# Start offsets of SBUF tiles: three unused tiles ahead of the large ones in a Griffin-style encoder layer

## The chip, the cores and the metric

The kernel runs on one core of one Trainium2 chip. The metric is the device time of one execution in microseconds (us). Five engines work from their own instruction streams: TensorE (PE; its weight loads are listed apart as PEld), VectorE (DVE), ScalarE (ACT), GpSimd (POOL) and SyncE (SP), which here only issues transfers. SBUF has 128 partitions; a tile takes the same range of bytes in each of them, and "offset" below is where that range begins. Times are in us, durations of single instructions in ns.

## The reference

One layer over 1024 frames of width 1024, in float32: RMSNorm, one combined projection, two attention branches, a gated merge, an output projection and a squared-ReLU feed-forward, then a final RMSNorm.

```python
h = rms_norm(x, norm1[l])
proj = h @ w_in[l]
qa, ka, va, fa, qc, kc, vc, gates = jnp.split(proj, SPLITS, axis=-1)
o_a = forgetting_attention(qa, ka, va, cumsum(log_sigmoid(fa + forget_bias)))   # 8 heads x 64, causal
o_b = chunk_band_attention(qc, kc, vc, rel_bias)                                # 8 heads x 64, 640 keys
g_a, g_b = jnp.split(jax.nn.sigmoid(gates), 2, axis=-1)
merged = g_a * (o_a @ w_branch_a) + g_b * (o_b @ w_branch_b)
x = x + merged @ w_out
x = x + jnp.square(jax.nn.relu(rms_norm(x, norm2) @ w_up)) @ w_down             # 1024 -> 4096 -> 1024
return rms_norm(x, final_norm)
```

(Calls are shortened; head reshapes and casts are left out.)

## The kernel before

**Arithmetic.** Each float32 operand of a product is split into a high part, rounded to the matmul's float32r, and the low rest. A product is three matmuls of 128x128 weights with 128x512 moving columns: high x high, low x high, high x low (line 216). ScalarE makes the high part by a cast (lines 163 and 278), VectorE or GpSimd the low part by a subtraction (lines 165 and 279). The large projections use Strassen's scheme with seven products in place of eight, so sums and differences of weights (names S, ks, ka) and of activations (T1 to T4) are formed too.

**Stages.** Opening: x is loaded in tiles of 128x512 (xg), scaled, split and combined into the operands B11 to T4, while the first gates and the forget projection f are multiplied; the same x, laid out by rows, is loaded into the tiles n0, n1 and the two halves of rstd in turn and squared (line 312) for the first norm. Then the projections of q, k, v and the gates (to about 420 us), attention over 16 heads (to about 650 us; scores s from qk and sk, exponentials p, transposes pt, their parts th and tl, weighted sums pv), the branch and output projections, the up projection with its activations stored to DRAM (to about 1112 us), and the down projection, which reads them back, with the final norm and the output.

**Order of work.** A scheduler at build time puts the instructions of each engine in order, from the program and a model of durations; operations called through the wrappers VO, TO, AO, GO, LO keep the order of the program (line 106 in the profile). In attention strings of letters (FOX_HEAD and the like) set the order by hand. Each engine runs its stream in order and waits on semaphores; SP, ACT and POOL each have a queue of transfers, all served by the same 16 DMA engines.

**Where tiles lie.** Pools are opened on one of two sides. Those on the left are stacked upward from the low end of SBUF, those on the right downward from the top, and a pool that is closed gives its range to the next one opened on its side. A tile begins where the tile before it in its pool ends, rounded up to 32 bytes. Left: cpool (constants and rstd, line 117), tp (eight temporary tiles of 2048 bytes, line 118), then the operands, etile and, in the down projection, the raw and split activations, weights and sums. Right: wp (weights raw and split, line 119, open to the end), then the tiles of the q, k, v stage (epb) and all of attention (aps, apq0, app, apq1, apv, ap0). Tiles of 512 bytes and more are multiples of 256 bytes long, so one small tile early in a stack sets the offset, modulo 256, of all that follow. cpool holds an unused tile of 128 bytes, gap, just ahead of rstd. Offsets of the tiles of 512 bytes or more, modulo 256:

| tiles | offset before |
|---|---|
| left side after cpool: tp (tmp, z, m, vt), xg, B11 to T4, u, zt, qk, v and at, xB, xT, ka, ks, acc | 224 |
| right side: wp (wr, wh, wl, S), epb (qkh, qkl, vs), bc, mh and ml | 224 |
| right side, attention from wide downward: wide, qk and sk operands, p, v, th, tl, on, lo, mv, rb | 32 |
| rstd | 192 |
| ident | 128 |

The weights of the forget projection are the exception within a tile: 40 columns each, 160 bytes apart in one slice of T4h (line 380), so the eight of them start at eight different offsets.

Of the kernel before, what the change touches and what calls it, by code (L numbers as in the profile page):

```python
# [11 lines left out]
F32 = mybir.dt.float32  # L12
# [6 lines left out]
P = 128  # L19
# [73 lines left out]
def hybrid_block(ctx: ExitStack, tc: tile.TileContext, xT, xN, g1, wall, wf, fb, relb, g2, g3, outT):  # L93
# [17 lines left out]
    def pool(stack, name, side, bufs=1, **kw):  # L111
        return stack.enter_context(tc.tile_pool(name=name, bufs=bufs, side=side, reuse_waits="tile", **kw))
# [3 lines left out]

    cpool = pool(ctx, "cpool", "left")
    tp = pool(ctx, "tp", "left")
    wp = pool(ctx, "wp", "right")
    dpool = ctx.enter_context(tc.tile_pool(name="dpool", bufs=1, space=DRAM))  # L120

# [12 lines left out]

    cpool.tile([P, 32], F32, tag="gap", name="gap")
    rstd = cpool.tile([P, S], F32, tag="rstd", name="rstd")

    def dram(name, shape, dt=F32):
        return dpool.tile(shape, dt, tag=name, name=name)
# [510 lines left out]
    bstack.close()  # L650
    aps = pool(astack, "aps", "right")
    wide = aps.tile([P, S], F32, tag="wide", name="wide")
    G.memset(wide, 0.0)
    G.affine_select(out=wide[:, S - P:S], in_=wide[:, S - P:S], compare_op=ALU.is_ge, fill=-BIG, base=0, pattern=[[-1, P]],
                    channel_multiplier=1)
# [691 lines left out]
```

## Time and profile before

| | |
|---|---|
| median of 3 runs | 1427.92 us (1427.64 to 1430.43) |
| profiled execution, its own time | 1430.48 us |
| its span, first to last instruction | 1428.5 us |
| granted TensorE clock, mean | 0.995 |
| instructions in the span | 20411 |
| moved to and from DRAM | 259.75 MB in 132820 packets, mean 182 GB/s |

The span is what the profile covers; 2.0 us of the execution's own time lie around it. A group's row in the profile gives line, engine, operation, output <- inputs, shape and count, then busy time and mean of one, then the idle time ahead of it and who ended that. A matmul's duration there is its way through the array, and successive matmuls overlap: what the next one waits for is the distance of their starts. Rows that begin with minimum/median/maximum come from the view of one line or one tile.

### The profile page before, as it was taken

What the parts mean: (1) busy time and instruction counts of PE and PEld (TensorE: products, weight loads), DVE (VectorE), ACT (ScalarE), POOL (GpSimd) and SP (SyncE); (2) the same over time, 40 slices, a digit from 0 to 9 for tenths busy, and PEclk for the clock granted to TensorE, in tenths of its full rate; (3) what the DMA queues carried; (4) which work ended last, traced back from release to release, by engine and by line L of the source; (5) the groups of instructions that cost most, each with busy time, mean ns of one, the idle gap of its engine ahead of it and who ended that gap; (6) DMA issues with size and microseconds to landing.
All of it is one profiled execution on the core that took longest, in us unless ns stands there. A gap on an engine that the chain in (4) does not pass through costs nothing.

```text
span 1428.5 us, 20411 instructions
## 1 busy us (share of the span) xinstructions
PE 1400.7 (98%) x6676; PEld 1168.7 (82%) x6676; DVE 885.1 (62%) x1389; ACT 706.6 (49%) x1361; POOL 812.2 (57%) x639
## 2 busy tenths in 40 slices
PE   9999999999999999999999999999999999999996
PEld 6788888888878888888888888888888888888885
DVE  7756445543258887776655855545555559998644
ACT  8534333343358887775454543333333444444653
POOL 0477777778832233113724677777777545567564
PEclk9999999999999999999999999999999999999998
DMA  8546667773454668886644244444444784678263
GB/s 282 154 116 194 187 196 219 204 198 121 147 169 147 185 209 248 246 257 215 213 162 146 68 166 151 155 154 157 148 154 169 252 269 156 178 234 225 81 221 118
DMA packets 132820, 259.75 MB, mean 182 GB/s; under 512 B 18594, under 2 KB 20642, under 8 KB 129642
## 3 DMA queue, kind: packets, MB, share of 16 engines
q1 hardware_dynamic: 84570, 172.79, 38.6%
q10 hardware_dynamic: 44944, 77.78, 17.2%
q0 software_dynamic: 3200, 7.88, 2.5%
q8 instruction: 52, 0.85, 0.2%
q14 instruction: 54, 0.44, 0.1%
HBM read 172.70 MB, written 85.69 MB: 181 GB/s over the span
## 4 chain that ended last, share of the span: by engine, by line
PE 87%; DVE 3%; issue 3%; ACT 2%; POOL 2%; DMA 2%; SPq 0%; POOLq 0%; ACTq 0%; DVEq 0%
PE u L216 44%; PE dS L216 12%; PE dA L216 5%; PE o L216 5%; PE s L106 5%; PE pv L106 4%; PE pt L106 3%; PE m L106 3%; PE m L216 3%; POOL wl_A L165 1%; PE u L106 1%; DMA xg<-xT 1%; DMA xT<-a_dram 1%; ACT p L106 1%; PE vtp L627 0%
## 5 line engine op out<-in xcount | busy, mean ns | idle before, releaser
L165 POOL TENSOR_TENSOR wl_A<-wr,wh_A 128x512 fp32r<-128x512 f32 x118 | 158.4, 1352 | 94.0 <-ACT wh_A L163 77.0
L165 POOL TENSOR_TENSOR wl_S<-S,wh_S 128x512 fp32r<-128x512 f32 x102 | 136.0, 1337 | 32.9 <-ACT wh_S L163 32.3
L163 ACT CAST wh_S<-S 128x512 fp32r<-128x512 f32 x105 | 64.6, 621 | 114.0 <-PE u L216 53.9
L163 ACT CAST wh_A<-wr 128x512 fp32r<-128x512 f32 x105 | 65.0, 620 | 88.7 <-PE u L216 55.8
L106 DVE TENSOR_TENSOR tl<-pt,th 128x512 fp32r<-128x512 f32 (+1 forms) x144 | 90.5, 641 | 25.9 <-ACT th L106 24.4
L165 POOL TENSOR_TENSOR wl_S<-ks,wh_S 128x512 fp32r<-128x512 f32 x48 | 69.1, 1501 | 53.4 <-ACT wh_S L106 50.0
L590 DVE TENSOR_TENSOR u<-u,u 128x512 f32<-128x512 f32 x70 | 48.8, 698 | 76.0 <-PE u L216 73.6
L106 ACT ACTIVATE p<-s,mn 128x640 f32<-128x640 f32 (+3 forms) x120 | 84.4, 703 | 16.6 <-DVE mn L106 15.5
L106 ACT CAST th<-pt 128x512 fp32r<-128x512 f32 (+1 forms) x144 | 77.6, 551 | 24.5 <-PE pt L106 22.3
L106 PE MATMUL pt<-ident,p 128*128 128x128 f32 x528 | 78.1, 274 | 1.2 <-DVE zt L403 1.1
L186 POOL TENSOR_TENSOR S<-wr,wr 128x512 f32<-128x512 f32 x35 | 46.3, 1324 | 54.8 <-DMA wr<-wall 50.2
L106 PEld LDWEIGHTS pt<-ident,p 128*128 128x128 f32 x528 | 62.2, 141 | 11.0 <-PE pv L106 2.0
L106 PE MATMUL s<-qk 128*128 128x384 f32 (+2 forms) x192 | 58.6, 360 | 8.1 <-ACT p L106 7.3
L165 POOL TENSOR_TENSOR wl_A<-ka,wh_A 128x512 fp32r<-128x512 f32 x32 | 45.1, 1419 | 35.6 <-ACT wh_A L106 34.1
L278 ACT CAST qkh<-qk 128x512 fp32r<-128x512 f32 x32 | 19.9, 621 | 87.5 <-DMA qk_dram<-qkl 34.2
L1102 ACT ACTIVATE v<-v 128x512 f32<-128x512 f32 x64 | 40.4, 632 | 45.1 <-DVE v L1101 42.9
L924 POOL TENSOR_TENSOR on<-on,lo 128x512 f32<-128x512 f32 x7 | 9.0, 1292 | 92.7 <-ACT lo L106 92.7
L106 PE MATMUL pv<-th,v 128*128 128x512 f32 (+3 forms) x180 | 61.3, 348 | 0.1
L583 DVE TENSOR_TENSOR u<-u,c 128x512 f32<-128x512 f32 x35 | 24.5, 699 | 59.4 <-PE u L216 57.3
L106 PE MATMUL pv<-tl,v 128*128 128x512 f32 (+3 forms) x180 | 56.8, 335 | 0.2 <-DVE tl L106 0.2
L1101 DVE SCALAR_TENSOR_TENSOR v<-u,rstd 128x512 f32<-128x512 f32 x64 | 43.9, 688 | 20.1 <-PE u L216 18.1
L581 DVE TENSOR_TENSOR c<-u,u 128x512 f32<-128x512 f32 x35 | 24.2, 691 | 50.7 <-PE u L216 48.9
(445 smaller groups left out, 4742.2 us busy)
## 6 DMA issues: line engine op xcount, KB each, us to landing
wr<-wall SPq DMA_DIRECT2D x233, 256.0 KB
a_dram<-at ACTq DMA_DIRECT2D x64, 256.0 KB
xT<-a_dram SPq DMA_DIRECT2D x64, 256.0 KB
qk<-qk_dram SPq DMA_DIRECT2D x15, 1024.0 KB
qk_dram<-qkh ACTq DMA_DIRECT2D x96, 128.0 KB
a_dram<-v ACTq DMA_DIRECT2D x48, 256.0 KB
xB<-a_dram SPq DMA_DIRECT2D x44, 256.0 KB
z_dram<-zt ACTq DMA_DIRECT2D x32, 256.0 KB
```

Of the source, the lines that this page charges most:

```text
L106: return lambda *a, **kw: tc.keep_in_program_order(getattr(self.eng, name)(*a, **kw))
L163: (act.tensor_copy if act is G or act is V else act.copy)(wh, src)
L165: lows.append(eng.tensor_tensor(wl, src, wh.bitcast(F32), op=ALU.subtract))
L186: eng.tensor_tensor(t, raw(3), raw(2), op=ALU.add)
L216: done = eng.matmul(bank, w[wi], x[xi], start=(first and t == 0), stop=(t == n - 1 and not part), skip_group_check=part or not first)
L278: A.copy(dst[0], src)
L581: V.tensor_tensor(c22, banks[2], u2, op=ALU.add)
L583: V.tensor_tensor(banks[1], banks[3], c22, op=ALU.add)
L590: V.tensor_tensor(banks[b], banks[b], u2, op=ALU.add)
L924: G.tensor_tensor(o, o, lows_o[pr], op=ALU.add)
L1101: V.scalar_tensor_tensor(v, src, 0.0, rstd[:, hs(h)], op0=ALU.max, op1=ALU.mult)
L1102: A.activation(v, v, AF.Square)
```

## The change

Three tiles that nothing uses are added. A pool "edge" with 96 bytes (24 float32) is opened on the right ahead of wp, so that it lies at the top of SBUF; cpool gets 32 bytes (8 float32) behind rstd; aps gets 64 bytes (16 float32) behind wide.

```diff
     cpool = pool(ctx, "cpool", "left")
     tp = pool(ctx, "tp", "left")
+    pool(ctx, "edge", "right").tile([P, 24], F32, tag="shim", name="shim")
     wp = pool(ctx, "wp", "right")
...
     cpool.tile([P, 32], F32, tag="gap", name="gap")
     rstd = cpool.tile([P, S], F32, tag="rstd", name="rstd")
+    cpool.tile([P, 8], F32, tag="shim", name="shim")
...
     aps = pool(astack, "aps", "right")
     wide = aps.tile([P, S], F32, tag="wide", name="wide")
+    aps.tile([P, 16], F32, tag="shim", name="shim")
```

Left tiles behind rstd move up by 32 bytes, right tiles move down by 96, and those from wide downward by 96 + 64 = 160. In the two programs every instruction, its place on its engine, its semaphores and the counts that it waits for are the same; the SBUF offsets in the operands are what differs. Modulo 256 they become:

| tiles | before | after |
|---|---|---|
| left side after cpool | 224 | 0 |
| right side | 224 | 128 |
| attention from wide downward | 32 | 128 |
| rstd | 192 | 192 |
| ident | 128 | 128 |

Modulo 128, then, all large tiles stand at 0 but rstd, which stands at 64. The small tiles of cpool and aps behind the new ones (sums of the norms, minima and denominators of the softmax) move by 32, 96 or 160 bytes as well.

## The prediction

> **What bounds the kernel now.** I read the busy times first, then the chain of waits, then the stages one by one. The page's first part and its chain:
>
> ```profile
> PE 1400.7 (98%) x6676; PEld 1168.7 (82%) x6676; DVE 885.1 (62%) x1389; ACT 706.6 (49%) x1361; POOL 812.2 (57%) x639
> PE 87%; DVE 3%; issue 3%; ACT 2%; POOL 2%; DMA 2%; SPq 0%; POOLq 0%; ACTq 0%; DVEq 0%
> PE u L216 44%; PE dS L216 12%; PE dA L216 5%; PE o L216 5%; PE s L106 5%; PE pv L106 4%; PE pt L106 3%; PE m L106 3%; PE m L216 3%; POOL wl_A L165 1%; PE u L106 1%; DMA xg<-xT 1%; DMA xT<-a_dram 1%; ACT p L106 1%; PE vtp L627 0%
> ```
>
> TensorE is busy for 98% of the span and is 87% of the chain. All other engines and the transfers share the remaining 13%. The stages say where that rest lies (columns: duration, busy time and instructions of PE, its weight loads, DVE, ACT, POOL, then granted clock, DMA share, GB/s):
>
> ```profile
> 0.00:50.00 50.00, 44.83 (x187) 33.44 (x188) 41.62 (x76) 40.75 (x85) 3.28 (x8) 1.00 0.66 224
> 330.00:440.00 110.00, 106.04 (x494) 87.83 (x494) 48.82 (x91) 50.15 (x98) 62.42 (x51) 0.98 0.46 147
> 440.00:900.00 460.00, 453.39 (x2406) 386.61 (x2404) 326.35 (x603) 282.44 (x588) 202.00 (x153) 1.00 0.60 187
> 900.00:1000.00 100.00, 100.00 (x443) 82.84 (x442) 49.13 (x68) 38.56 (x64) 77.14 (x59) 1.00 0.45 153
> 1180.00:1428.00 248.00, 236.62 (x1088) 196.94 (x1086) 183.95 (x217) 117.85 (x211) 143.89 (x111) 0.98 0.57 173
> ```
>
> Between 900 and 1000 us PE never pauses. The pauses are 5.2 us in the opening, 4.0 us where attention begins, 6.6 us in the 460 us after that, and 11.4 us in the last stretch, most of it the tail after the last products. So a change can reach the end in two ways only: by what a matmul itself takes, or through about 28 us of pauses.
>
> **The change part by part.** *The three tiles.* Nothing writes or reads them, so they issue no instruction. The order of instructions, the semaphores waited on and the counts waited for are the same in both programs on all five engines; buffers are numbered differently, and the start offsets in SBUF differ. No step is moved past a queue and no wait is added. Direct cost: 0 us. What is left is the offsets. Tiles on the left side stood at 224 modulo 256 and come to 0; those on the right at 224 or (attention) 32, and come to 128; the 4 KB tile rstd stays at 192, so "all large tiles" is one short. The question is whether any instruction or transfer sees that. Tiles at 32, 192 and 224 already work side by side, and comparing them is the nearest thing the trace has to the change.
>
> *TensorE.* Its weight is the largest: every nanosecond on each of 6676 matmuls is 6.7 us (6676 x 1 ns). Two stretches, one with all operands at 224 (the up projection) and one with operands at 32 (scores in attention), columns being start, duration, engine and line:
>
> ```profile
> 1000.05 0.39 PE L216 MATMUL u<-T1h,wl_S 128*128 128x512 f32 x1
> 1007.08 0.39 PE L216 MATMUL u<-B22h,wh_S 128*128 128x512 f32 x1
> 605.36 0.39 PE L106 MATMUL s<-qk 128*128 128x512 f32 x1
> 605.59 0.39 PE L106 MATMUL s<-sk 96*128 96x512 f32 x1
> 605.82 0.38 PE L106 MATMUL pt<-ident,p 128*128 128x128 f32 x2
> ```
>
> From 1000.05 to 1007.08 there are 31 steps, so one matmul starts every 0.227 us; at 605.36 the steps are 0.23 and 0.23. Start offset 32 and start offset 224 give one pitch within the 10 ns that these rows resolve on a single step. Weight loads say the same, at 32 (v), at 224 (wh_g), and for 40-column slices of T4h that lie 160 bytes apart and so start at 224, 128, 32, 192, 96, 0 and on modulo 256:
>
> ```profile
> L106 PEld LDWEIGHTS pv<-th,v 128*128 128x128 f32 x180 | 34.0, 189 | 3.3 <-ACT th L106 0.3
> L371 PEld LDWEIGHTS g<-B21h,wh_g x8: 187/188/188, 16.3 to 22.5; 128*128 128x128 f32 x8
> L386 PEld LDWEIGHTS f<-B22h,T4h x4: 114/114/114, 26.8 to 37.9; 128*40 128x40 f32 x4
> L386 PEld LDWEIGHTS f<-B12l,T4h x4: 115/115/116, 25.2 to 36.3; 128*40 128x40 f32 x4
> ```
>
> 189 against 188 ns, and 114 to 116 ns for offsets that include 0 and 128, the two that the change brings. I take 0 ns for a matmul. As bounds I keep one nanosecond either way, which is the difference of the two full weight loads: -6.7 to +6.7 us.
>
> *ScalarE, VectorE, GpSimd.* One line squares tiles n (224) and rstd (192) in turn; on DVE and on POOL an operation with one or two SBUF operands stands at 32 (on) and at 224 (z, wl_ab) (minimum, median, maximum in ns):
>
> ```profile
> L312 ACT ACTIVATE n<-n x8: 614/625/635, 20.8 to 36.3; 128x512 f32<-128x512 f32 x8
> L312 ACT ACTIVATE rstd<-rstd x8: 615/624/635, 22.6 to 39.0; 128x512 f32<-128x512 f32 x8
> L106 DVE TENSOR_TENSOR on<-pv,mv x16: 677/683/696, 437.1 to 647.2; 64x512 f32<-64x512 f32 x16
> L106 DVE TENSOR_TENSOR z<-m,z x16: 680/681/692, 552.7 to 661.7; 128x512 f32<-128x512 f32 x16
> L873 POOL TENSOR_TENSOR on<-on,rb x14: 1267/1290/1306, 451.8 to 633.5; 128x512 f32<-128x512 f32 x14
> L757 POOL TENSOR_TENSOR wl_ab<-wrab,wh_ab x8: 1270/1292/1297, 535.7 to 648.9; 128x512 fp32r<-128x512 f32 x8
> ```
>
> The medians differ by 1 ns of 625, 2 of 683 and 2 of 1290, at most 0.3%. These engines are 3 + 2 + 2 = 7% of the chain, 100 us; 0.3% of that is 0.3 us, either way. I take 0. What hides the rest of their work is TensorE's 87%; where that cover is missing, the 28 us of pauses, it would cost 0.1 us.
>
> *Transfers.* In the opening SP issues two loads of 256 KB into n (224), then two into rstd (192); counted through the queue at 128 packets of 2 KB a tile, the packets of n run from 18.2 to 19.6 us and those of rstd from 19.5 to 20.9. The transfers within 18.3 to 19.4 and within 19.6 to 20.8:
>
> ```profile
> 15.05 1.00 SPq L106 DMA_DIRECT2D n<-xN  x2
> 16.41 1.01 SPq L106 DMA_DIRECT2D rstd<-xN  x2
> DMA packets 234, 0.42 MB, mean 384 GB/s; under 512 B 28, under 2 KB 28, under 8 KB 234
> DMA packets 253, 0.46 MB, mean 384 GB/s; under 512 B 28, under 2 KB 28, under 8 KB 253
> ```
>
> 384 GB/s for both, with the engines full. A start on a multiple of 64 (192) is worth nothing over one on 32 (224). No large transfer in this trace starts at 0 or 128, so this stays a bound: the nearest row says 0%. The far end goes by how many blocks a row of 2048 bytes touches: off a boundary of 128 it is 17 blocks in place of 16 (1/17, 6%), off a boundary of 256 it is 9 in place of 8 (1/9, 11%), and the latter is mended for left tiles alone, since right ones come to 128. The chain holds 2% of transfers, 29 us, so the far end is -3.2 us; a loss has no mechanism in these rows, and I keep the same 3.2 us for it. I take 0.
>
> *Sum.* 0 + 0 + 0 + 0 = 0. The profiled execution took 1430.48 us (span 1428.5 and 2.0 around it) and stands 2.56 us above the median of the three runs shown, 1427.92. No change to the one is no change to the other: **1427.9 us**.
>
> **The rivals.**
>
> *Transfers see a boundary* (faster). For it: every large transfer now starts off both boundaries, and afterwards only those of rstd start off 128. Against a boundary of 128: nothing direct, but n and rstd are equal although only rstd stands on a multiple of 64. Against one of 256: nothing, since n and rstd both miss it. Times: with 128 bytes 1427.9 - 1.7 = 1426.2, within 0.2%; with 256 bytes, if every transfer on the chain is one of the left side, 1427.9 - 3.2 = 1424.7, just beyond.
> The Trainium skill, page "DMA: Bandwidth & Descriptors", section "How a descriptor splits into AXI transactions", has a rule that speaks for the change: a transaction that reads must begin on a multiple of 256 bytes, and a descriptor that does not is charged the bytes before its start. As an estimate from that page, and if it held for the SBUF side of loads as well, 2048 bytes would cost 71 beats at 224, 70 at 192, 68 at 128 and 64 at 0, so left transfers would shorten by 10% and right ones by 4%. By that rule n and rstd should differ by 1.4%; the two rows above show no difference, though that is near what so short a window can tell.
>
> *TensorE streams faster from an aligned start* (faster). The mechanism: a matmul's fixed part contains a fetch that an aligned start saves. For it: 512 columns start every 0.227 us and 256 columns every 0.12, as the two ends of three steps near the end show, so 0.013 us of each matmul is fixed (2 x 0.12 - 0.227):
>
> ```profile
> 1414.86 0.28 PE L106 MATMUL dA<-xT4l,wh_A 128*128 128x256 f32 x1
> 1415.22 0.28 PE L106 MATMUL dA<-xT4l,wh_A 128*128 128x256 f32 x1
> ```
>
>  Against it: it is the same pitch at 32 and 224, and the T4h slices load in one time at every offset. Each nanosecond saved is -6.7 us; from 0.43 ns on it shows (2.86 / 6.7). With 1 ns: 1421.2 us.
>
> *Both sides meet on one weight port* (slower). Left tiles move to 0, right tiles to 128, while both stood at 224; the moving operand comes from the left and the weights from the right. If a load of weights and the stream under it then disturb each other, the weight load of 188 ns grows. It is hidden under the matmul before it until it passes 227 ns, so it decides from +39 ns; each nanosecond beyond is +6.7 us, and 1 ns beyond gives 1434.6 us. Against it: weight loads from v (32), wh_g (224) and the T4h slices show no dependence on where the two stand to each other.
>
> *It doesn't do what it says.* rstd keeps 192, and it is read by every scaling on DVE. If rstd alone carried the cost, nothing would move: 1427.9 again, the same number for another reason.
>
> **How the numbers follow.** What a measurement can tell here is about 0.2%, 2.86 us; the three runs shown lie 2.79 us apart. No effect at all, with rstd's case: 0.67, at 1427.9, own range 1425.5 to 1430.5. Transfers with 128 bytes 0.06 (same), with 256 bytes 0.06 (faster). TensorE faster: 0.09. Weight port: 0.06 (slower). The remaining 0.06 is for offsets that act through something I have not named: 0.02 faster, 0.04 slower, since no row excludes a loss there. Sums: faster 0.06 + 0.09 + 0.02 = 0.17; same 0.67 + 0.06 = 0.73; slower 0.06 + 0.04 = 0.10. The range takes in the transfers' gain and their loss, and most of TensorE's bound on the side of the gain: 1422.5 to 1431.5 us. Left out are the weight port, part of the unnamed and the far part of TensorE's gain, together under 0.2.
>
> **What would show it.** Right: 6676 matmuls and the same 0.227 us pitch; weight loads at 188 ns; ACT at 620 to 625 ns for 128x512 squares from a tile that now stands at 0; the xN loads still at 384 GB/s into n and rstd alike; the chain still 87% PE. Wrong: a pitch that is not 0.227 (TensorE), a rate for n that parts from rstd's (transfers, decided by n at 0 or 128 against rstd at 192 in one trace), or weight loads over 190 ns. A time outside 1425.1 to 1430.8 with all those rows equal would mean that offsets act through something that I have not named.

## The result: slower by 1.6%

| | before | after |
|---|---|---|
| median | 1428.66 us (1427.64 to 1430.43) | 1451.97 us (1450.48 to 1452.36) |
| profiled execution, span | 1428.5 us | 1448.6 us |
| granted TensorE clock, mean | 0.995 | 0.997 |

(Medians of five runs each.) After over before is 1.0158, with a 95% interval from 1.0146 to 1.0169: 23.3 us more by the medians, 20.1 us more by the two spans. The profiled execution of before, 1430.48 us, was its longest, and that of after, 1450.48 us, its shortest, which makes the 3.2 us between the two differences. The forecast was 1427.9 us, 1422.5 to 1431.5.

The page of the profile after, its busy times and its chain of waits:

```profile
PE 1421.5 (98%) x6676; PEld 1167.8 (81%) x6676; DVE 889.0 (61%) x1389; ACT 706.2 (49%) x1361; POOL 809.4 (56%) x639
PE 88%; DVE 4%; issue 3%; ACT 2%; POOL 1%; DMA 1%; SPq 0%; POOLq 0%; ACTq 0%; DVEq 0%
```

PE's busy time has grown by 20.8 us, with the same 6676 matmuls. Its weight loads, ACT and POOL have not grown, and DVE's 3.9 us lie beside PE. The 100 us of the up projection in which PE never pauses (columns as in the prediction) now hold 434 matmuls in place of 443, at the full clock:

```profile
900.00:1000.00 100.00, 100.00 (x434) 81.20 (x433) 48.84 (x67) 38.06 (x63) 74.22 (x57) 1.00 0.42 148
```

To place the time I cut both spans at the same matmuls, from the first of a stage to the first of the next, and took in each stage the mean distance from one start of a 512-column matmul to the next, over the distances below 260 ns (longer ones hold a pause or a record that is missing):

| stage | matmuls | before, us | after less before, us | distance before, ns | after, ns |
|---|---|---|---|---|---|
| opening | | 37.15 | +0.20 | | |
| projections of q, k, v, gates | 1630 | 363.76 | +8.54 | 227.0 | 233.1 |
| first scores | | 18.02 | +0.11 | | |
| attention | 1454 | 244.50 | -1.64 | | |
| branch projections | 192 | 43.60 | +1.25 | 226.8 | 233.3 |
| out projection | 384 | 87.04 | +0.02 | 226.7 | 226.7 |
| up projection | 1376 | 310.85 | +6.02 | 226.7 | 231.6 |
| down projection | 1411 | 313.30 | +5.68 | 226.7 (dS) | 232.4 (dS) |

Four stages lose 21.5 us, and the out projection, built in the same way with weights that are split in the same way, loses nothing. (The down projection of before holds one pause of about 1.3 us, at 1406 us where PE waits for wl_A, which the profile after has not, nor those with all tiles at 0 and at 128; without it the four lose 22.8 us, near the 23.3 of the medians.) Its rows are the control. The groups of one form, before and then after (the last numbers are busy time, mean ns of one, and the idle time ahead of it):

```profile
L216 PE MATMUL u<-T4h,wh_A 128*128 128x512 f32 x136 | 52.9, 389 | 0.0
L216 PE MATMUL o<-mh,wh_o 128*128 128x512 f32 x128 | 49.8, 389 | 0.0
L216 PE MATMUL dS<-xT1l,wh_S 128*128 128x512 f32 x64 | 24.9, 389 | 0.0
```

```profile
L218 PE MATMUL u<-T4h,wh_A 128*128 128x512 f32 x136 | 53.5, 394 | 0.0
L218 PE MATMUL o<-mh,wh_o 128*128 128x512 f32 x128 | 49.8, 389 | 0.0
L218 PE MATMUL dS<-xT1l,wh_S 128*128 128x512 f32 x64 | 25.2, 395 | 0.0
```

389 ns becomes 394 and 395, except for o. The timeline of after shows what that means for the next matmul:

```profile
760.01 0.39 PE L218 MATMUL o<-ml,wh_o 128*128 128x512 f32 x1
763.87 0.39 PE L218 MATMUL o<-mh,wh_o 128*128 128x512 f32 x1
1200.31 0.40 PE L218 MATMUL dS<-xT1h,wh_S 128*128 128x512 f32 x1
1203.81 0.40 PE L218 MATMUL dS<-xT1h,wh_S 128*128 128x512 f32 x1
```

Seventeen steps of the out projection take 3.86 us, 0.227 each; fifteen of the down projection take 3.50 us, 0.233 each. The longer steps are not in a few matmuls that wait. In the projections, the branch and the down projection hardly one step in a thousand is still at 227 ns or below, and they follow a regular pattern (down projection: 228, 230, 233, 241, 232, 231, 232 ns and so on). In the up projection 12% are.

Now the front's table of offsets explains which stage is which. The moving operand of the out projection, mh and ml, lies on the right, like the weights: both went from 224 to 128 together. In the other four stages it lies on the left and came to 0, while the weights came to 128; only the operands of k = 3 in the up projection, all but those of B11, lie on the right too (line 1073 of before), which the table does not list. In before they had stood at one offset, 224.

### The profile page after: what moved, and what is told of

Its sections match the earlier page's. It is cut to its first block, busy times and chain, and to the rows that moved or that the text cites. A ratio compares the mean times of both kernels' runs of the same rounds, so it can differ in the third digit from the quotient of the medians.

```text
span 1448.6 us, 20411 instructions
## 1 busy us (share of the span) xinstructions
PE 1421.5 (98%) x6676; PEld 1167.8 (81%) x6676; DVE 889.0 (61%) x1389; ACT 706.2 (49%) x1361; POOL 809.4 (56%) x639
## 4 chain that ended last, share of the span: by engine, by line
PE 88%; DVE 4%; issue 3%; ACT 2%; POOL 1%; DMA 1%; SPq 0%; POOLq 0%; ACTq 0%; DVEq 0%
PE u L218 45%; PE dS L218 12%; PE dA L218 5%; PE o L218 5%; PE s L106 4%; PE pv L106 4%; PE pt L106 3%; PE m L106 3%; PE m L218 3%; POOL wl_A L167 1%; PE u L106 1%; DMA xg<-xT 1%; DMA xT<-a_dram 1%; ACT p L106 1%; DVE xg L332 1%
## 5 line engine op out<-in xcount | busy, mean ns | idle before, releaser
L106 ACT ACTIVATE p<-s,mn 128x640 f32<-128x640 f32 (+3 forms) x120 | 84.2, 702 | 16.0 <-DVE mn L106 15.1
L167 POOL TENSOR_TENSOR wl_S<-wr,wh_S 128x512 fp32r<-128x512 f32 x34 | 45.1, 1326 | 24.8 <-ACT wh_S L165 24.8
```

What stands on the lines that cost most here:

```text
L106: return lambda *a, **kw: tc.keep_in_program_order(getattr(self.eng, name)(*a, **kw))
L167: lows.append(eng.tensor_tensor(wl, src, wh.bitcast(F32), op=ALU.subtract))
```

## The experiments

After this comparison there were two theories. **Pair:** a matmul slows down when its moving operand and its weights start at different offsets modulo 256. **Absolute:** some offset of the change, 0 or 128, is bad by itself, or the attention tiles or ident are. In the edits below the added tiles of the change are named by their bytes: "top" lies above the weights' pool wp, "behind wp" is a tile in a second pool on the right opened just after wp, "behind rstd" is in cpool. Of runs with an interval, the ratio is to the kernel before on the same chip; the others are one execution each, timed beside it.

### One tile at the top

Only the right side moves, by 128 bytes. All offsets modulo 128 are those of before, so nothing is better or worse aligned to 128; left and right differ by 128 (224 against 96).

```diff
+    pool(ctx, "edge", "right").tile([P, 32], F32, tag="shim", name="shim")
     wp = pool(ctx, "wp", "right")
```

> Edit: the kernel before with one unused tile of 128 bytes at the top of the right side and nothing else; every tile keeps its offset modulo 128, while left and right side come to differ by 128 modulo 256 (left 224, right 96, attention 160). Theory A (a matmul is slowed when the offset of its moving operand and that of the weights differ modulo 256): the projections, branch, up and down stages lose what they lost in the changed kernel, 8.5 + 1.3 + 6.0 + 5.7 = 21 us, the output projection (both operands on the right) nothing, and the time is about 1450 us. Theory B (a start on multiples of 128 itself is slow): nothing stands on multiples of 128 that did not before, 1428.7 us. Theory C (a moving operand at 0 modulo 256 is slow, at 224 and 128 not): 1428.7 us.

Measured: 1452.07 us, ratio 1.0160 (1.0147 to 1.0173). Projections +7.42, branch +1.08, out projection +0.05, up +6.25, down +6.07 us. This is the whole loss of the change without its alignment.

### Everything at 0, everything at 128

The change with one of its sizes altered: 224 bytes at the top in place of 96, so that the right side comes to 0 like the left; and 160 bytes behind rstd in place of 32, so that the left side comes to 128 like the right.

```diff
-    pool(ctx, "edge", "right").tile([P, 24], F32, tag="shim", name="shim")
+    pool(ctx, "edge", "right").tile([P, 56], F32, tag="shim", name="shim")
```

> Edit: the changed kernel with 224 bytes in place of 96 at the top of the right side; all large tiles but rstd and ident stand at 0 modulo 256, so also on multiples of 128, and left and right do not differ. Theory A: the matmuls of all dense stages start every 227 ns again, about 1428.7 us, with attention within 2 us either way. Theory B: as slow as the changed kernel or slower, 1452 us, the output projection slow too if 0 is worse than 128. Theory C: 1452 us and more, since the output projection's moving operand stands at 0 now too.

```diff
-    cpool.tile([P, 8], F32, tag="shim", name="shim")
+    cpool.tile([P, 40], F32, tag="shim", name="shim")
```

> Edit: the changed kernel with 160 bytes in place of 32 behind rstd; all large tiles but rstd stand at 128 modulo 256, ident as well. Theory A: dense stages at 227 ns a matmul as before, and attention 1.6 us shorter as in the changed kernel, where p, its transposing identity, th and v first stood at one offset: about 1427 us. Theory B: 1452 us as the changed kernel. Theory C: 1427 us.

Measured: 1428.34 us, ratio 0.9994 (0.9985 to 1.0002), and 1427.36 us, ratio 0.9992 (0.9984 to 1.0001). From the groups of the first and of the second kernel, and 31 steps in the first one's timeline (7.03 us, 0.227 each):

```profile
L218 PE MATMUL u<-T4h,wh_A 128*128 128x512 f32 x136 | 53.0, 389 | 0.0
L218 PE MATMUL dS<-xT1l,wh_S 128*128 128x512 f32 x64 | 24.9, 389 | 0.0
...
999.80 0.39 PE L218 MATMUL u<-T3h,wh_S 128*128 128x512 f32 x1
1006.83 0.39 PE L218 MATMUL u<-B22l,wh_S 128*128 128x512 f32 x1
```

```profile
L218 PE MATMUL u<-T4h,wh_A 128*128 128x512 f32 x136 | 52.9, 389 | 0.0
```

Neither 0 nor 128 is bad by itself, and neither is good: with both sides on a multiple of 256 the time is that of 224 on both sides. "Absolute" falls for the large products. From before to either kernel the two sides have moved by 256 bytes against each other (32 up and 224 down; 160 up and 96 down) and nothing is lost, so 256 is a period of the effect.

### The weights alone

A tile at the top and one behind wp that together are 256 bytes move wp (weights raw and split, and their sums S) and nothing else. Now the out projection has to lose as well, since its mh and ml stay at 224.

```diff
+    pool(ctx, "edge", "right").tile([P, 32], F32, tag="shim", name="shim")
     wp = pool(ctx, "wp", "right")
+    pool(ctx, "edge2", "right").tile([P, 32], F32, tag="shim", name="shim2")
```

> Edit: the kernel before with 128 unused bytes above wp and 128 below it, so that only the weights (wr, wh, wl, S) move, from 224 to 96 modulo 256, and every other tile keeps its offset modulo 256. Theory A: the stages of the changed kernel are slow (21 us), and the output projection as well, 384 matmuls of 87 us in all, by about 5 ns each, 2 us: 1451 to 1453 us. If instead the slowing came from the other engines' traffic on the right side meeting TensorE's, and not from the weights: the output projection stays at 87.0 us. Theories B and C: 1428.7 us.

Measured: 1455.39 us. The out projection takes 2.20 us more (projections +9.38, branch +1.07, up +6.42, down +6.08), and its group of matmuls is now at 395 ns. Its weight loads (minimum, median, maximum) are where they were:

```profile
L218 PE MATMUL o<-mh,wh_o 128*128 128x512 f32 x128 | 50.5, 395 | 0.0
L218 PEld LDWEIGHTS o<-mh,wh_o x128: 187/188/192, 717.9 to 806.4; 128*128 128x128 f32 x128
```

So it is not the load of the weights that is stretched; by the records it is the stream of columns. (The end of a matmul's record is modelled; the distance of the starts is measured.)

### What stands against the weights: the matmul's own operand, or other engines' writes

ACT and POOL write split weights all the time, and they moved with wp too. An unused tile between the raw and the split weights inside wp leaves wh, wl and S at 224, and moves the raw weights and all that lies below on the right: mh and ml come to 96.

```diff
     def split_w(src, name, act=A, eng=G):
+        if not rawgap:
+            rawgap.append(wp.tile([P, 32], F32, tag="shim", name="shim"))
         wh = wp.tile([P, HALF], F32R, tag="wh", name=f"wh_{name}", bufs=HL)
```

> Edit: the kernel before with an unused tile of 128 bytes between the raw weights wr and the split weights in wp: wh, wl and S keep 224, while wr and everything further down on the right (epb, bc, mh and ml, attention) move by 128. Here TensorE's weights and its left-side operands agree, and what the other engines read and write on the right differs from both. Theory A with TensorE's own two reads as the colliding pair: projections, branch and down projection as before; the output projection, whose moving operand mh, ml now stands at 96 against weights at 224, +2.2 us; the up projection +1 to 2 us, for the operands of k = 3 that stand on the right; in all about 1432 us. Theory A' (the other engines' accesses to the right side collide with TensorE's reads on the left): 1450 us.

Measured: 1434.01 us. Projections -0.33, branch +0.02, down -1.25 us: no loss where the moving operand is on the left at 224. Out projection +2.55, and up +2.64, where a part of the operands is on the right.

```profile
L220 PE MATMUL o<-mh,wh_o 128*128 128x512 f32 x128 | 50.6, 395 | 0.0
L220 PE MATMUL dS<-xT1l,wh_S 128*128 128x512 f32 x64 | 24.9, 389 | 0.0
```

The same weights at the same place are slow under mh at 96 and fast under xT1l at 224. The out projection's weights, besides, are written by 16 casts of 0.62 us and 16 subtractions of 1.35 us, at most 31.4 of its 89.6 us, and yet all its steps but one are late, at 229 to 238 ns. The pair is TensorE's own: the columns that stream, and the weights. That the weights meet the stream while they are loaded for the next matmul is a reading; no run separates it.

### The curve of the difference

Six more places for the weights, with the two tiles of 8 and 56, 16 and 48, 48 and 16, 56 and 8, 24 and 40, 40 and 24 float32 in place of 32 and 32.

> Edit: the kernel before with the weights alone (wr, wh, wl, S) moved by 32 bytes, from 224 to 192 modulo 256. Theory A1 (any difference between moving operand and weights modulo 256 costs the same): the dense stages lose what they lost with 128, some 26 us with the output projection, 1455 us. Theory A2 (the cost grows with the distance up to 128): a quarter, about 6 us, 1435 us. Theory A3 (a difference below 128 is harmless, only the opposite half of 256 collides): 1429 us.

> Edit: the weights alone moved by 64 bytes, from 224 to 160 modulo 256. A1: 1455 us. A2: half, about 13 us, 1442 us. A3: 1429 us.

> Edit: the weights alone moved by 192 bytes, from 224 to 32 modulo 256, which is 64 ahead of the moving operands where the run with 160 stood 64 behind. If the distance alone counts: the same time as the run with 160. If it counts which of the two lies ahead: another time, and the weights being loaded during the stream of the matmul ahead of them would be the reason to look at the order of the accesses.

> Edit: the weights alone moved from 224 to 0 modulo 256, 32 ahead of the moving operands; 32 behind cost 233.3 ns a matmul in place of 226.7. If every difference but 0 costs something: between 229 and 233 ns a matmul in the output projection, 1438 to 1458 us. If only some differences collide (those of 64 behind cost a third of the others): this one can be free, 1429 us.

> Edit: the weights alone moved from 224 to 128 modulo 256, 96 behind the moving operands. If every difference but 0 costs something: 229 to 233 ns a matmul in the output projection, 1438 to 1458 us; if the cost of 64 behind (228.9 ns) is the low end of a valley between 32 and 128 behind, near that, 1438 us; if some differences are free, 1429 us.

> Edit: the weights alone moved from 224 to 64 modulo 256, 96 ahead of the moving operands, the last distance in steps of 32 that is not measured. Weights less moving operand so far, in ns from one matmul's start to the next in the output projection: 0 gives 226.7; 32, 64, 160 and 224 give 233.3; 128 gives 232.4; 192 gives 228.9. If equality alone is free and 192 is the one cheap difference: 232 to 233.3 ns, 1455 to 1459 us. If distances come in cheap pairs around 128 or 0: 229 ns, 1438 us.

The out projection is the cleanest stage, since all its moving operands stand at one offset. The time of the whole kernel holds the other stages too, whose moving operands lie on the left. Offset of the weights less that of the moving operand, modulo 256:

| difference | weights at, moving at (out projection) | whole kernel, us | out projection, us more | distance of starts, ns |
|---|---|---|---|---|
| 0 | before 224, 224; after 128, 128; one tile at the top 96, 96; all at 0 | 1428.66; 1451.97; 1452.07; 1428.34 | 0 to 0.05 | 226.7 to 226.8 |
| 32 | 0, 224 | 1458.78 | 2.56 | 233.3 |
| 64 | 32, 224 | 1456.64 | 2.56 | 233.3 |
| 96 | 64, 224 | 1462.51 | 2.92 | 234.3 |
| 128 | 96, 224 | 1455.39 | 2.20 | 232.4 |
| 128 | 224, 96 | 1434.01 | 2.55 | 233.3 |
| 160 | 128, 224 | 1456.31 | 2.56 | 233.3 |
| 192 | 160, 224 | 1437.96 | 0.85 | 228.9 |
| 224 | 192, 224 | 1458.13 | 2.56 | 233.3 |

The count of matmuls in one stretch of 80 us, all but about 1 us of it in the out projection, with the weights at 192, 160 and 64:

```profile
720.00:800.00 80.00, 80.00 (x345) 64.26 (x344) 42.63 (x59) 36.90 (x63) 28.96 (x21) 1.00 0.46 150
720.00:800.00 80.00, 80.00 (x351) 65.63 (x350) 48.64 (x65) 40.64 (x70) 28.25 (x21) 1.00 0.42 138
720.00:800.00 80.00, 80.00 (x343) 64.33 (x342) 40.66 (x56) 35.69 (x62) 28.65 (x21) 1.00 0.44 149
```

It is not a matter of how far the two stand apart, nor of half a period: every difference but 0 costs 5.7 to 7.6 ns a matmul, save 192, which costs 2.2. A1, which has one cost for every difference, comes nearest and misses 192; A2 and A3 fall at 32 bytes. 64 behind costs 2.2 ns and 64 ahead 6.6, so it counts which of the two lies ahead. The difference does not settle the cost to the last ns either: 128 costs 5.7 with the weights at 96 and 6.6 with the weights at 224. The last run, at 96, came out above its forecast of 1455 to 1459 us. The smallest step that the pools allow, 32 bytes, costs as much as 160. The down projection of the kernels with weights at 0, 32, 64, 128 and 192 is 6.6 to 8.1 us longer than before, that with 160 only 1.4.

### The transposes' ident

In attention the transposes take p at 32 and ident at 128; ident alone was brought to 32.

```diff
+    cpool.tile([P, 40], F32, tag="shim", name="shim")
     ident = cpool.tile([P, P], F32, tag="ident", name="ident")
+    cpool.tile([P, 24], F32, tag="shim2", name="shim2")
```

> Edit: the kernel before with 160 unused bytes ahead of ident and 96 behind it, so that ident alone moves, from 128 to 32 modulo 256, where the exponentials p stand that it transposes (p is the weights, ident the moving operand). If the 1.6 to 1.8 us that attention gained in the changed kernel and with everything at 128 came from ident and p standing at one offset: attention 242.8 us in place of 244.5, nothing else moved, about 1427 us. If they came from attention's tiles standing on multiples of 128: 244.5 us and 1428.9 us.

Measured: 1428.33 us, ratio 0.9993 (0.9984 to 1.0001); attention -1.44 us in its first 35 us and +0.98 later. No gain that can be told: the theory that this pair matters falls, for transposes of 128 columns between waits.

It left the 1.6 us by which attention is shorter in the profile after. They are at one place. Around the start of attention in before, at the same work in after, and in the kernel with everything at 128 (the last three columns are granted clock, DMA share, GB/s):

```profile
427.00:431.00 4.00, 3.58 (x14) 3.34 (x15) 2.96 (x8) 2.98 (x8) 0.00 (x0) 0.57 0.35 131
```

```profile
435.50:438.50 3.00, 2.22 (x14) 2.03 (x15) 2.53 (x7) 2.62 (x7) 0.00 (x0) 1.00 0.46 175
```

```profile
427.00:431.00 4.00, 4.00 (x26) 3.46 (x26) 3.53 (x8) 3.65 (x9) 0.00 (x0) 1.00 0.30 115
```

The same 14 matmuls run with a clock of 0.57 in before and at the full clock in after, which makes about 1.4 us. The dip stands in the profiles of nine of the fourteen kernels at this place, whatever their offsets, and not in four (the change, all at 128, weights at 32, weights at 128); the one with ident at 32 has it later, between 500 and 545 us, where the mean clock is 0.96. It goes with no offset and so is taken for chance and not for an effect of the change, though no run shows it in one execution of a kernel and not in another, since each has one profile. It hides 1.4 us of the loss in a comparison of these two spans; without it and without the pause of 1.3 us they would be 22.8 us apart, as the four stages say.

## Why the prediction was wrong, point by point

**What bounds the kernel** held: a change in what a matmul takes reaches the end in full. PE's busy time grew by 20.8 us and the span by 20.1.

**The step that failed** is the one on TensorE, "I take 0 ns for a matmul. As bounds I keep one nanosecond either way". It measured +4.9 ns from start to start in the up projection (226.7 to 231.6), +5.7 in the down projection and +6.1 in the projections, so the bound was too small by a factor of five or six. Over the 4609 matmuls of the four stages (1630 + 192 + 1376 + 1411; a few are narrower), 21.5 us are 4.7 ns each. Behind it stood the sentence that comparing tiles at 32, 192 and 224 "is the nearest thing the trace has to the change". It was not. In before, the up projection has both its operands at 224 and the scores have both at 32: the rows compare two absolute offsets at one difference, which is zero. What the change alters is the difference, from 0 to 128, and no row that I quoted had another one in dense matmuls of 512 columns. The table of offsets showed it: two sides both at 224 before, 0 and 128 after. A bound of 1 ns, taken from two weight loads that differed by 1 ns, said nothing about a case that neither of them was.

One row of the trace of before seemed to be at hand. The forget projection streams 512 columns against slices of T4h that lie at eight offsets, in the opening, where the gates run with both operands at 224:

```profile
L386 PE MATMUL f<-B12h,T4h x4: 397/398/398, 25.2 to 36.3; 128*40 128x512 f32 x4
L371 PE MATMUL g<-B21h,wl_g x8: 388/389/393, 18.1 to 23.1; 128*128 128x512 f32 x8
L371 PE MATMUL g<-B12h,wl_g x8: 387/392/398, 24.3 to 36.1; 128*128 128x512 f32 x8
```

398 against 389 ns. I read the weight loads of f, 114 to 116 ns, and not the matmuls over them. But the row does not show the effect: the first of its four has both operands at 224 and took 398 as well, and in the same microseconds g<-B12h,wl_g, at 224 on both sides, took up to 398. The trace of before held no clean price for a difference.

**The slower rival** had the right two operands, left and right, meeting at different offsets, and the wrong place. It put the cost on the weight load, to be felt "from +39 ns". The load stayed at 188 ns, and the distance of the matmuls' starts grew instead, which is felt from the first nanosecond, since nothing covers it. Its price of 6.7 us for each nanosecond over all 6676 matmuls was of the right kind, with 0.06 on it.

The Trainium skill, page "SBUF — State Buffer", section "Who interferes with whom", gives PE two independent read ports, one for the moving operand and one for the weights. These runs do not agree: wherever the two offsets differ modulo 256, a matmul of the out projection takes 2.2 to 7.6 ns more.

**Transfers.** The term, 0 us, held; the row behind it did not, and the test of n against rstd could not decide. In after n stands at 0 and rstd still at 192. The two stretches of the prediction, in after and then in the kernel with everything at 0:

```profile
DMA packets 243, 0.45 MB, mean 410 GB/s; under 512 B 23, under 2 KB 23, under 8 KB 243
DMA packets 265, 0.49 MB, mean 408 GB/s; under 512 B 26, under 2 KB 26, under 8 KB 265
```

```profile
DMA packets 243, 0.44 MB, mean 399 GB/s; under 512 B 29, under 2 KB 29, under 8 KB 243
DMA packets 269, 0.49 MB, mean 406 GB/s; under 512 B 31, under 2 KB 31, under 8 KB 269
```

410 and 408, 399 and 406 GB/s, against 384 and 384 in before, 389 and 388 with one tile at the top, 382 and 382 with everything at 128. The rate goes with the left side: in the two kernels where it stands at 0 each packet of 2 KB in these stretches takes 84 ns, in the twelve others 87.6 to 88.3 in the mean. (The loads of after run half a microsecond earlier: counted as in the prediction, those into n from 17.7 to 19.0 us and those into rstd to 20.3.) So an offset of 0 is worth some 4% of a packet where the transfers fill the engines. The kernel with the weights alone at 0 shows it within one trace: the loads into n and rstd, at 224 and 192, take 87.8 ns, and of the four loads of raw weights behind them, at 0, the last three take 84.0; in before these four, at 224, take 87.6 to 88.3. The stores between 900 and 1000 us take 84.2 and 84.1 ns in the two kernels with the left side at 0, and 86.2 to 87.2 in the others. In after the loads into rstd at 192 and into the weights at 128 run at 84 as well, between loads at 0, so the pace belongs to the run of loads and not to one tile; why, no run tells. In time it brings nothing that can be told: everything at 0 has the ratio 0.9994 (0.9985 to 1.0002). The rival that transfers see a boundary of 256 bytes was right about the transfers and wrong about its price of 3.2 us.

By the prediction's estimate from the Trainium skill, page "DMA: Bandwidth & Descriptors", section "How a descriptor splits into AXI transactions", a start at 0 would cost 64 beats and one at 224 would cost 71, 10% less; the trace agrees in the direction, with 84 against 88 ns on the loads, and not in the size.

**ScalarE** stands within 1% of the forecast, 620 to 625 ns, at 0 (n) as at 192 (rstd):

```profile
L314 ACT ACTIVATE n<-n x8: 615/626/636, 20.3 to 36.1; 128x512 f32<-128x512 f32 x8
L314 ACT ACTIVATE rstd<-rstd x8: 621/630/640, 22.0 to 38.7; 128x512 f32<-128x512 f32 x8
```

VectorE and GpSimd add nothing to the chain beyond 1% more for DVE and 1% less for POOL.

**"TensorE streams faster from an aligned start"** is wrong: 226.7 ns with all at 0, with all at 128 and with all at 224.

**What would show it wrong** named "a pitch that is not 0.227 (TensorE)". That is the row that spoke. The xN loads "still at 384 GB/s" did not stay there either, without a cost in time.

## What to carry to other kernels

Where a kernel is bound by dense matmuls, put the moving operand and the weights of each product at the same SBUF offset modulo 256; a small tile at the head of one pool sets or spoils that for a whole side, and alignment as such brought no time here. Look for it in the distance from start to start within a long run of equal matmuls: 0.227 against 0.233 us for 512 columns is 1.6% of a kernel that is 98% busy, and no wait, idle time or weight load tells of it; the matmul's own row does, with 389 against 394 ns. When a trace is searched for the price of a new placement, compare pairs that differ as the new pair will, not two pairs whose members agree.

## What the runs showed of the hardware

- The distance of the starts of 512-column matmuls depends on the difference of the operands' start offsets modulo 256: 226.7 to 226.8 ns at 0, 232.4 to 234.3 at 32, 64, 96, 128, 160 and 224, and 228.9 at 192. Which part of the memory or of its ports makes it so, why 192 is cheap, and whether another dtype or width behaves alike, no run here tells. The difference of 192 was measured once, with the weights at 160. The kernels that move the weights alone were run once each.
- The weight load of 188 ns, 187 to 192 at the most, does not show it, though the weights are one of the two partners.
- Where transfers fill the engines, a packet of 2 KB takes 84 ns in kernels whose left side stands at 0 modulo 256 and 87.6 to 88.3 ns on the mean in the others, in the same stretch of the opening.
- A granted clock of 0.57 for some 4 us where attention begins stands in nine of fourteen profiles, one of each kernel, whatever the offsets, and is worth 1.4 us, half of the 2.8 us between the shortest and the longest run of before.
